# A head step, a kept-weights step, the mixer's bank pairs and the first tiles put in another order in a one-core decoder layer

## The chip, the cores and the metric

The kernel runs on one core of one Trainium2 chip. The metric is the device time of one execution in microseconds (us). The core's engines are named as in its profile: PE (matrix products), PEld (its weight loads), DVE (vector), ACT (scalar, pointwise functions), POOL (general purpose) and SP, which issues most DMAs. Each engine takes its instructions strictly in order.

## The reference

One layer of a decoder on 1040 rows (16 learned rows ahead of 1024 tokens) of 1024 columns, in float32:

```python
u = rmsnorm(h, mix_norm_pre[l])
proj = u @ w_in[l]
q, f_logit, i_in, g_out, v_pool, gate_a, gate_b = jnp.split(proj, cuts, axis=-1)
a = hgrn2(q, f_logit, i_in, g_out, lbs[l], hgrn_out_norm[l])
p = multiscale_pool(v_pool, pool_proj[l], pool_scale[l])
z = (sigmoid(gate_a) * (a @ w_branch_hgrn[l])
     + sigmoid(gate_b) * (p @ w_branch_pool[l]))
h = h + rmsnorm(z @ w_out[l], mix_norm_post[l])
u = rmsnorm(h, ffn_norm_pre[l])
gt = causal_dwconv(u @ ffn_w_gate[l], ffn_conv_w[l], ffn_conv_b[l])
y = (gelu(gt) * (u @ ffn_w_up[l])) @ ffn_w_down[l]
h = h + rmsnorm(y, ffn_norm_post[l])
```

`hgrn2` is a gated linear recurrence over four heads of 128 columns, `multiscale_pool` subtracts each value from trailing means over 2, 4, 8 and 16 rows and multiplies each of four groups by a 128x128 matrix.

## The kernel before

**Products.** Every float32 operand is split into two parts that PE takes at its faster float32 rate: a rounded high part (a cast, on ACT, names ending in `hi` or `h`) and the rest (a subtraction, on DVE, names ending in `lo` or `l`). A product is then three matmuls, high by high, high by low and low by high (`mm3`, lines 221 to 223; in `proj_parts`, lines 241, 242 and 245). So each weight goes DRAM, `wraw`, ACT, DVE, PE, and an operand is ready only when its low part is.

**Stages.** The first tiles (lines 1060 to 1170, to about 60 us): rows of the input are loaded, squared and summed on ACT (`sq`), scaled on DVE (`scaled`, into `un`), transposed on PE (`turn`, line 1097, into a bank `pt`, four 128x128 pieces each), split (`hi_` on ACT, `lo_` on DVE) and multiplied with the columns of `w_in` for the value projection (`mm_`, into the two banks `pv`). The 1024 inner columns are taken as eight groups of 128 (0 to 7, the last arguments of `hi_`, `lo_` and `mm_`); a `turn` makes four groups of one row tile, and the weights come as four blocks of two groups each (`wi_hi`, `wi_lo`; `ha` and `hb` are the two halves of a block). Ahead of it `warm(n)` issues n products of constants (`pj`, line 534) into a bank that nobody reads, and a small transpose (`pp`, line 1070) makes the gains `gcol`. This part is ordered by hand for ACT, DVE and PE: what stands in the code stands so on each engine. After row tiles 0 and 1 the next rows are transposed at line 455.

Then the gates (to about 325 us), the heads and the branch products (325 to 554), the mixer `z @ w_out` (554 to about 655) and the feed-forward part (to the end).

**Heads and branches.** For PE this stage is ordered by hand, by the string `ORDER` (line 56); DVE, ACT and POOL are placed by a scheduler that follows what PE needs. A name in `ORDER` is one item: `h0` to `h3` are the next step of that head's generator `head_steps` (line 690); `PV`, `G` and `PP` are projections (`PP` the pooled ones, product bank `ppp`, evacuated by DVE into `uhi`); `BB` and `BA` are the products of the pooled and of the recurrent branch, 8 column groups each (banks `pbb` and `pba`, evacuated into `sa`), where `a` and `b` are the halves of a product whose inner columns are cut in two; `sa0` to `sa3` split a head's output into `ah` and `al`, the operands of `BA`; `w0` to `w5` each run a step of `keep_first` or `keep_unit`.

A head step begins with a multiply on DVE of every second row of `q` by `f` (line 753), then 32 small products `kb` by `q` into a bank `sb` (line 758), then levels: 32 small products into `sl` (line 735), the last ones `sm` (line 774) and `ms` (lines 837, 838, sums for a normalization).

**Kept weights.** `keep_unit` (line 986) loads two blocks of a feed-forward weight ahead of its stage, forms the sums that a seven-product (Strassen) scheme needs on DVE, splits them (ACT `whi`, DVE `wlo`) and writes the result to DRAM as `kept...`, from where the feed-forward stage loads it. The step numbers: the first makes P1 and P2, the next P6 and P5, the third P3 and P7, the fourth P4.

**Banks.** PSUM has eight banks here. `bank()` takes the next free one of the pool, so where a product lies depends on which tiles were taken ahead of it, and its first matmul waits until the tile that had the bank is evacuated. The mixer stage takes the banks in pairs (`pair`): `R[i]` is a row tile's pair, `m` that of the two learned rows that are needed. At the last BA product a `spare` bank is taken and written once by DVE.

The few lines that the prediction's steps need:

```python
    def warm(n):
        for _ in range(n):
            pe.matmul(junk_bank[:, :P], onesm, ident, start=True, stop=True)
...
        q2, f2 = (t[:, M0:].rearrange("p (b two) -> p b two", two=2) for t in (q, f))
        dve.tensor_tensor(q2[:, :, 1], q2[:, :, 1], f2[:, :, 1], ALU.mult)
        ps = bank("sb")
...
            if (kind, i) == ("BA", KD - 1):
                dve.memset(bank("spare")[:, :1], 0.0)
                z0 = [split_z(0, k) for k in range(ZA)]
...
        for i in (1, "m", 0):
            R[i] = Row(0 if i == "m" else HALO + i * P, HALO if i == "m" else P, pair("pm"))
```

## Time and profile before

| what | us |
|---|---|
| median of 3 runs (1304.87 to 1306.25) | 1305.03 |
| the profiled execution | 1304.06 |
| its span, first to last instruction | 1302.4 |
| PE busy | 1287.9 |
| DVE busy | 963.0 |
| ACT busy | 526.8 |
| POOL busy | 354.1 |

A row of the timeline reads: start and duration in us, engine, line of the code, operation, output <- inputs, shapes, and how many instructions stand together; in brackets how long the engine was idle ahead of it and what ended that. Line 81 is a helper through which all DVE and ACT operations go, so there the names tell the place. Starts of PE's matmuls overlap the end of the one ahead, so that the time of a product is the distance of starts, not its duration. The profiled execution's time is 1.66 us longer than its span; the span is what the rows add up to.

### The profile page before, as it was taken

Reading aid. Unit: us, or ns where it says so; the run is one execution under the profiler, and the core shown is the slowest. Engines: PE = TensorE matmul, PEld = TensorE weight load, DVE = VectorE, ACT = ScalarE, POOL = GpSimd, SP = SyncE. Lnnn points to the kernel's source line nnn. Section 1 sums busy time; section 2 is a strip of 40 time slices with the busy share of each in tenths; the row PEclk is TensorE's granted clock in tenths of the full one; section 3 lists DMA queues with packets and bytes.
Section 4 is the critical chain, followed back from the end, with each engine's and each line's share of the span. In section 5 each row is a group of like instructions: output and inputs, shape, how many; then the busy total and the mean of one; then the engine's idle time right before and its main releaser. Section 6 shows DMA issues by size and latency. Waiting matters only on the chain.

```text
span 1302.4 us, 21989 instructions
## 1 busy us (share of the span) xinstructions
PE 1287.9 (99%) x8651; PEld 1136.6 (87%) x8651; DVE 963.0 (74%) x1312; ACT 526.8 (40%) x918; POOL 354.1 (27%) x308
## 2 busy tenths in 40 slices
PE   8999999999999999999999999999999999999998
PEld 7799899999999898968898888888888888888887
DVE  6768965554776878766688999888898885455758
ACT  7554533332244646235563222222232232444443
POOL 3015333130000000150145555454665552000000
PEclk9999999999999999999999999999999999999999
DMA  7145542325614767866777776667777699666644
GB/s 279 42 107 170 196 158 97 122 90 157 175 61 145 228 227 259 308 194 243 275 251 250 206 212 173 160 184 199 179 177 171 146 262 287 208 226 222 231 170 162
DMA packets 143817, 247.62 MB, mean 190 GB/s; under 512 B 11008, under 2 KB 75180, under 8 KB 143714
## 3 DMA queue, kind: packets, MB, share of 16 engines
q1 hardware_dynamic: 127026, 213.42, 49.1%
q0 software_dynamic: 12064, 24.38, 11.3%
q10 hardware_dynamic: 4624, 8.41, 1.7%
q8 instruction: 68, 1.11, 0.4%
q14 instruction: 35, 0.29, 0.1%
HBM read 174.12 MB, written 95.09 MB: 207 GB/s over the span
## 4 chain that ended last, share of the span: by engine, by line
PE 93%; DVE 2%; ACT 2%; DMA 1%; issue 0%; SPq 0%; POOL 0%; DVEq 0%; ACTq 0%; POOLq 0%
PE P L341 17%; PE P L342 17%; PE P L344 17%; PE pd L221 5%; PE pd L223 5%; PE pd L222 5%; PE pm L221 2%; PE pm L223 2%; PE pm L222 2%; PE ppv L241 1%; PE ppv L245 1%; PE ppv L242 1%; PE pg L241 1%; PE pv L223 1%; PE pg L242 1%; PE pv L221 1%
## 5 line engine op out<-in xcount | busy, mean ns | idle before, releaser
L81 ACT CAST whi<-wraw 128x512 fp32r<-128x512 f32 (+2 forms) x140 | 97.0, 714 | 163.6 <-PE P L342 87.7
L342 PE MATMUL P<-v,whi 128*128 128x512 f32 (+2 forms) x408 | 140.7, 353 | 0.0
L341 PE MATMUL P<-v,whi 128*128 128x512 f32 (+2 forms) x408 | 140.7, 352 | 0.0
L344 PE MATMUL P<-v,wlo 128*128 128x512 f32 (+2 forms) x424 | 135.1, 349 | 0.0
L81 DVE TENSOR_TENSOR p<-p,P 128x512 f32<-128x512 f32 (+2 forms) x122 | 83.3, 683 | 44.1 <-PE P L344 43.2
L81 DVE TENSOR_TENSOR wlo<-wraw,whi 128x512 fp32r<-128x512 f32 (+2 forms) x110 | 95.9, 891 | 11.3 <-ACT whi L81 7.0
L312 POOL TENSOR_TENSOR swa<-wraw,wraw 128x512 f32<-128x512 f32 x32 | 49.3, 1540 | 188.6 <-DMA wraw<-in_w_in_dram 77.1
L81 DVE TENSOR_TENSOR rot<-wraw,rot 128x1024 fp32r<-128x1024 f32 x31 | 37.9, 1224 | 72.3 <-ACT rot L81 72.2
L341 PEld LDWEIGHTS P<-v,whi 128*128 128x128 f32 x408 | 76.7, 188 | 10.5
L342 PEld LDWEIGHTS P<-v,whi 128*128 128x128 f32 x408 | 76.6, 188 | 10.2
L344 PEld LDWEIGHTS P<-v,wlo 128*128 128x128 f32 x424 | 74.0, 188 | 10.8
L223 PE MATMUL pd<-rot 128*128 128x512 f32 x274 | 82.5, 388 | 0.0
L222 PE MATMUL pd<-rot 128*128 128x512 f32 x274 | 82.5, 388 | 0.0
L221 PE MATMUL pd<-rot 128*128 128x512 f32 x274 | 81.9, 388 | 0.1
L81 ACT CAST whi<-swa 128x512 fp32r<-128x512 f32 x64 | 38.1, 619 | 92.3 <-PE P L342 81.8
L81 DVE TENSOR_TENSOR wlo<-swb,whi 128x512 fp32r<-128x512 f32 x64 | 65.9, 1037 | 9.5 <-ACT whi L81 9.5
L81 ACT CAST rot<-wraw 128x1024 fp32r<-128x1024 f32 x31 | 32.7, 1054 | 90.8 <-PE pd L223 89.4
L341 PE MATMUL P<-uhi,whi 128*128 128x258 f32 (+2 forms) x240 | 68.5, 303 | 0.0
L342 PE MATMUL P<-ulo,whi 128*128 128x258 f32 (+2 forms) x240 | 68.4, 303 | 0.0
L81 ACT CAST whi<-swb 128x512 fp32r<-128x512 f32 x64 | 38.1, 618 | 69.3 <-PE P L342 63.3
L341 PE MATMUL P<-t4h,whi 128*128 128x258 f32 (+2 forms) x228 | 65.5, 304 | 0.0
L341 PE MATMUL P<-t2h,whi 128*128 128x258 f32 (+2 forms) x228 | 65.3, 304 | 0.2 <-DVE sg L81 0.2
(354 smaller groups left out, 3751.3 us busy)
## 6 DMA issues: line engine op xcount, KB each, us to landing
wraw<-in_w_in_dram SPq DMA_DIRECT2D x36, 512.0 KB, 5.6
yt<-ysum SPq DMA_DIRECT2D x33, 512.0 KB, 5.2
wraw<-in_ffn_w_gate_dram SPq DMA_DIRECT2D x26, 512.0 KB, 6.5
wraw<-in_ffn_w_up_dram SPq DMA_DIRECT2D x22, 512.0 KB, 6.9
wsum<-in_ffn_w_down_dram SPq DMA_DIRECT2D x22, 512.0 KB, 8.2
wraw<-in_w_out_dram SPq DMA_DIRECT2D x18, 512.0 KB, 6.1
ysum<-ys SPq DMA_DIRECT2D x11, 768.0 KB, 5.8
sa<-sscr SPq DMA_DIRECT2D x16, 513.0 KB, 7.5
```

Of the source, the lines that this page charges most:

```text
L81: self.last = method(*a, **k)
L221: pe.matmul(ps, ahi, bhi, start=first, stop=False)
L222: pe.matmul(ps, ahi, blo, start=False, stop=False)
L223: pe.matmul(ps, alo, bhi, start=False, stop=last)
L241: pe.matmul(ps[:, :n], whi[:, k, :], xhi, start=(k == 0), stop=False)
L242: pe.matmul(ps[:, :n], whi[:, k, :], xlo, start=False, stop=False)
L245: pe.matmul(ps[:, :n], wlo[:, k, :], xhi, start=False, stop=(k == n_k - 1))
L312: pool_e.tensor_tensor(s1, a21, a22, ALU.add)
L341: pe.matmul(d, whi[:, k, :], xh[:, c : c + w], start=(k == 0 and onto is None), stop=False, **go)
L342: pe.matmul(d, whi[:, k, :], xl[:, c : c + w], start=False, stop=False, **go)
L344: pe.matmul(x[:, o : o + w], wlo[:, k, :], xh[:, c : c + w], start=False, stop=(k == 3), **go)
```

## The change

Five edits, none of which changes what is computed:

1. *First tiles*: eleven junk products ahead of the small transpose and two behind it (eight and six before), the copy of `gcol` behind the scaling of row 0, and another order of casts, subtractions, transposes and products.
2. *Head steps*: for heads 0 and 1 the first multiply is issued ahead of the generator's first yield, that is one item earlier in `ORDER`.
3. `ORDER`: head 3's item between `PP3` and `BBa0` moves behind `BBa0`.
4. `ORDER`: a kept-weights step `w5` moves from ahead of `BBb6` to behind `BAa1` (it is the one with P3 and P7).
5. The `spare` bank at the last BA product is gone, and the mixer's pairs are taken in the order m, 0, 1.

```diff
-         "Gr3 h2 PP1 h0 Gs3 h3 PP2 h2 PP3 h3 BBa0 h1 h2 BBb0 h1 h3 w0 BBa1 h2 BBb1 h3 w1 BBa2 h2 BBb2 h3 w2 BBa3 h2 "
+         "Gr3 h2 PP1 h0 Gs3 h3 PP2 h2 PP3 BBa0 h3 h1 h2 BBb0 h1 h3 w0 BBa1 h2 BBb1 h3 w1 BBa2 h2 BBb2 h3 w2 BBa3 h2 "
...
+        q2, f2 = (t[:, M0:].rearrange("p (b two) -> p b two", two=2) for t in (q, f))
+        if h < 2:
+            dve.tensor_tensor(q2[:, :, 1], q2[:, :, 1], f2[:, :, 1], ALU.mult)
         yield
...
-        q2, f2 = (t[:, M0:].rearrange("p (b two) -> p b two", two=2) for t in (q, f))
-        dve.tensor_tensor(q2[:, :, 1], q2[:, :, 1], f2[:, :, 1], ALU.mult)
+        if h >= 2:
+            dve.tensor_tensor(q2[:, :, 1], q2[:, :, 1], f2[:, :, 1], ALU.mult)
...
-        warm(8)
+        warm(11)
         gp = bank("pp")
...
-        dve.tensor_copy(gcol, gp[:, :KD])
-        warm(6)
+        warm(2)
...
         sq(0)
         scaled(0, 0)
+        dve.tensor_copy(gcol, gp[:, :KD])
+        turn(0, 0)
         wi_hi(0, ha)
+        wi_hi(0, hb)
         wi_lo(0, ha)
-        turn(0, 0)
-        hi_(0, 0)
-        lo_(0, 0)
-        wi_hi(0, hb)
         wi_lo(0, hb)
-        hi_(0, 1)
-        lo_(0, 1)
+        hi_(0, 0, 1)
+        lo_(0, 0, 1)
         mm_(0, 0, 1)
...
-                dve.memset(bank("spare")[:, :1], 0.0)
...
-        for i in (1, "m", 0):
+        for i in ("m", 0, 1):
```

What the edits do to the order of instructions, at three places.

ACT in the first tiles, before (`un_228` is row 0's square, `whi_219` and `whi_221` are the first two weight blocks, `pt_237` and `pt_271` the first transposes of rows 0 and 1, `un_261` row 1's square):

```order
L81 CAST whi_219<-wiraw_94 128x512
L81 ACTIVATE uhi_90<-pt_237,gcol_211 128x128
L81 CAST whi_219<-wiraw_94 128x512
L81 ACTIVATE uhi_90<-pt_237,gcol_211 128x128
L81 ACTIVATE un_261,ssq_260<-row_96 128x1024
L81 ACTIVATE std_263<-ssq_260,eps_t 128x1
L81 ACTIVATE uhi_90<-pt_237,gcol_211 128x128 x2
L81 CAST whi_221<-wiraw_98 128x1024
L81 ACTIVATE uhi_90<-pt_271,gcol_211 128x128 x2
```

The same place after (`whi_217` and `whi_219` are now the first two blocks, `pt_234` and `pt_267` the transposes, `un_260` row 1's square):

```order
L81 CAST whi_217<-wiraw_94 128x512 x2
L81 ACTIVATE uhi_90<-pt_234,gcol_214 128x128 x2
L81 ACTIVATE un_260,ssq_259<-row_96 128x1024
L81 ACTIVATE std_262<-ssq_259,eps_t 128x1
L81 ACTIVATE uhi_90<-pt_234,gcol_214 128x128
L81 CAST whi_219<-wiraw_98 128x512
L81 ACTIVATE uhi_90<-pt_234,gcol_214 128x128
L81 CAST whi_219<-wiraw_98 128x512
L81 ACTIVATE uhi_90<-pt_267,gcol_214 128x128 x4
```

Both halves of the first block are cast ahead of row 0's groups 0 and 1, and the second block is cast half by half between its groups 2 and 3. On PE row 1's second transposes move behind two more groups of three products, and `mm_(0, 2)` and `mm_(0, 3)` now stand together ahead of `mm_(1, 0, 1)`.

DVE behind PP3, before (`ppp` are PP3's three banks, `sl_4980` head 3's moved products, `k_4552` and `q_4554` head 3's operands, `f_4375` head 2's):

```order
L81 SCALAR_TENSOR_TENSOR uhi_90<-ppp_4956,par,uhi_90 128x342
L81 TENSOR_TENSOR f_4375<-f_4375 128x66
L81 TENSOR_TENSOR k_4552<-k_4552,f_4551 128x132x4
L81 TENSOR_TENSOR q_4554<-q_4554,f_4551 128x128x4
L81 SCALAR_TENSOR_TENSOR uhi_90<-ppp_4957,par,uhi_90 128x342
L81 COPY_PREDICATED near_4701<-mask_155,sl_4980 128x32x4
```

And after (`sl_5005` is the same head step):

```order
L81 SCALAR_TENSOR_TENSOR uhi_90<-ppp_4956,par,uhi_90 128x342
L81 TENSOR_TENSOR f_4375<-f_4375 128x66
L81 SCALAR_TENSOR_TENSOR uhi_90<-ppp_4957,par,uhi_90 128x342
L81 TENSOR_TENSOR k_4552<-k_4552,f_4551 128x132x4
L81 TENSOR_TENSOR q_4554<-q_4554,f_4551 128x128x4
L81 COPY_PREDICATED near_4701<-mask_155,sl_5005 128x32x4
```

PP3's third evacuation moves ahead of two multiplies of head 3. On PE the 32 products of head 3 move from directly behind PP3 to behind the 18 products of BBa0. In the built program BBa0's banks are 6, 7 and 1 (before 7, 1 and 4); 6 is that of an earlier `sl` of head 3, 7 and 1 are PP2's first two, and 4 is PP2's third, which now goes to the moved `sl`. `sm` has bank 0, PP3's third.

DVE between the two splits of the last heads' outputs, before (`al_5840` and `al_5909` are the low parts of heads 2 and 3, `wlo_5755` and `wlo_5800` are kept weights, the latter P3 and P7, `wlo_5899` are the weights of BA2 and BA3, `pba_5914` is BA0's first bank):

```order
L81 TENSOR_TENSOR al_5840<-o_5593,ah_5839 128x1026
L81 TENSOR_TENSOR wlo_5755<-wlo_5755,whi_5754 128x512
L81 TENSOR_TENSOR wlo_5800<-wraw_5675,wraw_5677 128x512
L81 TENSOR_TENSOR wlo_5800<-wraw_5675 128x512
L81 TENSOR_TENSOR wlo_5755<-wlo_5755,whi_5754 128x512
L81 TENSOR_TENSOR al_5909<-o_5719,ah_5908 128x1026
L81 TENSOR_TENSOR wlo_5800<-wlo_5800,wraw_5675 128x512
L81 TENSOR_TENSOR wlo_5800<-wlo_5800,whi_5799 128x512
L81 TENSOR_TENSOR wlo_5800<-wraw_5677,wlo_5800 128x512
L81 TENSOR_TENSOR sa_5843<-sa_5843,pba_5914 128x342
```

And after (`al_5826`, `al_5895`, `wlo_5945` for P3 and P7, `wlo_5885` for BA2 and BA3, `pba_5900`):

```order
L81 TENSOR_TENSOR al_5826<-o_5593,ah_5825 128x1026
L81 TENSOR_TENSOR wlo_5755<-wlo_5755,whi_5754 128x512 x2
L81 TENSOR_TENSOR wlo_5885<-wraw_5883,whi_5884 128x1024
L81 TENSOR_TENSOR al_5895<-o_5719,ah_5894 128x1026
L81 TENSOR_TENSOR sa_5829<-sa_5829,pba_5900 128x342
L81 TENSOR_TENSOR sa_5829<-sa_5829,pba_5901 128x342
L81 TENSOR_TENSOR sa_5829<-sa_5829,pba_5902 128x342
L81 TENSOR_TENSOR wlo_5945<-wraw_5675,wraw_5677 128x512
```

The low part of BA2's and BA3's weights moves between the two `al`, and all of P3 and P7 moves behind BA0's evacuation. The six operations of P3 and P7 then stand among the evacuations of BA0 to BA2, and the low part of BA4's and BA5's weights, before ahead of BA2's evacuations, stands behind them.

At the seam to the mixer BA7's banks are 2, 6 and 7 (before 7, 5 and 1), and the pairs of the mixer's first rows are (0, 1) for row 0, (6, 7) for row 1 and (4, 5) for m; before, row 0 had (0, 1) too, with bank 1 still BA7's. For head 1's multiply of edit 2 the place on DVE is the same before and after, behind head 0's `f`; head 1's `k` moves behind the next multiply of `q` and the copy from `sb`.

28 lines of the change are left out of this document (15 added, 13 removed), and 4 rows, old and new, of the table ORDER.

## The prediction

> **What bounds the kernel now.** I read the page first, then the list of PE's waits, then the timelines of PE, DVE and ACT at each wait that the change can reach. The page (span; busy time of each engine):
>
> ```profile
> span 1302.4 us, 21989 instructions
> ...
> PE 1287.9 (99%) x8651; PEld 1136.6 (87%) x8651; DVE 963.0 (74%) x1312; ACT 526.8 (40%) x918; POOL 354.1 (27%) x308
> ```
>
> PE is busy in all but 14.5 us. The change takes no product away; it only reorders, so nothing but PE's waits can be won, and a reordering can lose by making new ones. What there is to win stands in the list of PE's waits (line waited for, us in total, times, longest):
>
> ```profile
> PE pba L242 <- DVE al L81: 1.1, 1, 1.1
> PE pbb L241 <- DVE uhi L81: 0.8, 1, 0.8
> PE pm L221 <- DVE sa L81: 0.7, 1, 0.7
> PE pba L245 <- DVE wlo L81: 0.6, 1, 0.6
> PE po L828 <- DVE st L81: 0.5, 2, 0.3
> PE sb L758 <- issue: 0.5, 1, 0.5
> PE pv L221 <- ACT uhi L81: 0.5, 1, 0.5
> PE pt L1097 <- DVE un L81: 0.4, 1, 0.4
> PE pv L223 <- DVE ulo L81: 0.3, 1, 0.3
> PE pv L222 <- DVE wlo L81: 0.2, 1, 0.2
> PE P L341 <- DVE sg L81: 0.2, 1, 0.2
> ```
>
> Each of these is one event of under 1.2 us (the `po` wait two), and together they are 5.8 us. The four `pv`/`pt` waits are the first tiles, `sb` is head 1's first step, `pbb` the first half of BBa0, the two `pba` the BA products, `pm` the mixer's first product; `po` and `P` (in the gates) are not touched. So the question is which of these go, and whether PE, coming earlier, waits for the same engine further on.
>
> **The change part by part.** *A, the first tiles.* PE's rows, and the ACT row from which the longest wait comes:
>
> ```profile
> 5.51 1.60 PE L534 MATMUL pj<-ident,onesm 128*128 128x128 f32 x12
> 8.01 0.50 PE L221 MATMUL pv<-whi,uhi 128*128 128x512 f32 x1 [0.46 <-ACT uhi L81]
> 10.97 0.63 PE L1097 MATMUL pt<-ident,un 128*128 128x128 f32 x4 [0.42 <-DVE un L81]
> 14.89 0.60 PE L1097 MATMUL pt<-ident,un 128*128 128x128 f32 x4
> 15.24 0.48 PE L221 MATMUL pv<-whi,uhi 128*128 128x512 f32 x1
> 22.16 0.39 PE L221 MATMUL pv<-wihi,uhi 128*128 128x512 f32 x1
> 22.84 0.60 PE L455 MATMUL pt<-ident,un 128*128 128x128 f32 x4
> 8.64 1.05 ACT L81 ACTIVATE un<-row 128x1024 f32<-128x1024 f32 x1
> ```
>
> From 22.16 to the transposes of line 455 stand three products, 22.84 - 22.16 = 0.68 us, so one takes 0.227. From 8.01 to 22.84, 14.83 us, stand 48 products (10.9 us) and three groups of four transposes (15.24 - 14.89 = 0.35 us each, 1.05): 12.0 us of work and 2.9 us of waits. In the new order the first product moves little, since the scaled half of row 0 and its transposes stay where they are: 7.9 rather than 8.01, as one small DVE copy now comes behind the scaling. Its six products and row 0's second transposes then run to about 9.6 with nothing between them, because both halves of the first weight block and both groups are split by then. The transposes of row 1 wait for the chain from ACT's square (8.64) over DVE's `un` to PE (10.97); ACT is free for it at 8.1 rather than 8.64, but when row 1's data land, no row shows, so I let it come only 0.1 us sooner: 10.87, a wait of 1.27. Of the next six products (groups 2 and 3) I charge waits of 0.55 us, since their two weight halves follow on ACT and DVE one by one. From there on (about 13.1) 36 products and the last transposes are back to back: row 1's groups 0 and 1 are split ahead, and each later split is put one group of products ahead of its use. The end: 7.9 + 12.0 + 1.27 + 0.55 = 21.7 rather than 22.84, a gain of **1.15 us**. The bounds: if the data of row 1 do not limit, the chain goes with ACT, 0.5 us more (1.65); if each of the three later splits comes a fifth of a microsecond late, 0.6 less (0.55). Nothing behind 22.84 is late next as far as PE's list shows: between here and the heads it has only the 0.2 us of `P`.
>
> The junk products `pj` ahead of it go from 14 to 13, two rather than six of them behind the small transpose. The later `pj` row takes 1.60 us for 12 records, 0.13 each, so the array is at speed before the first tile and products at 8 to 23 us take 0.227 like those at 22. [...]
>
> *B, head 0's and 1's first multiply issued ahead of the yield.*
>
> ```profile
> 334.10 0.75 PE L758 MATMUL sb<-q,kb 128*32 128x32 f32 x64 [0.49 <-issue]
> 333.31 0.69 DVE L81 TENSOR_TENSOR q<-q,f 128x512 f32<-128x512 f32 x1
> ```
>
> PE's `sb` of head 1 waits for DVE's `q<-q,f`, which ends at 334.0. In the order of DVE this multiply stands in the same place as before, directly behind head 0's `f<-f`; what moved is only head 1's `k<-k,f`, behind two of its neighbours. So the wait stays: **0**. The edit does not do there what its words say; the bounds are -0.2 (the `k` is needed by the next step) and the whole 0.5.
>
> *C, head 3's step behind BBa0.*
>
> ```profile
> 434.72 0.42 PE L241 MATMUL pbb<-uhi,whi 128*128 128x342 f32 x1 [0.78 <-DVE uhi L81]
> 438.24 0.24 PE L774 MATMUL sm<-q,k 128*16 128x1 f32 x4
> 439.24 0.42 PE L241 MATMUL pbb<-uhi,whi 128*128 128x342 f32 x1
> 432.39 0.57 DVE L81 SCALAR_TENSOR_TENSOR uhi<-ppp,par,uhi 128x342 fp32r<-128x342 f32 x1
> 438.27 0.57 DVE L81 SCALAR_TENSOR_TENSOR uhi<-ppp,par,uhi 128x342 fp32r<-128x342 f32 x1
> ```
>
> BBa0's third bank is the one that PP2's third evacuation (`uhi<-ppp`) frees, and PE stands 0.78 us for it. With head 3's 32 small products moved behind, `sl` takes that bank and BBa0 gets the one that head 3's earlier step left and PP2's first two. The last of these is free at 432.39 + 0.57 = 432.96, and PE asks for it about then. So that wait goes. What is late next is `sm`, 438.24 in before: its bank is now PP3's third, evacuated in before at 438.27. Two operations of head steps (a multiply of `k` and one of `q`, 0.6 us each as 512 columns take on DVE) come behind that evacuation instead of ahead of it, so it starts at 437.05 and ends at 437.6. `sm` then starts at about 437.6, and BBb0 as far behind it as before (439.24 - 438.24 = 1.0), at 438.6 rather than 439.24: **0.6 us** (0.2 if two thirds of one such operation still stand ahead; 0.95 if `sm` waits no more).
>
> *D, the kept-weights step moved from ahead of BBb6 to behind BAa1.*
>
> ```profile
> 509.72 1.22 DVE L81 TENSOR_TENSOR al<-o,ah 128x1026 fp32r<-128x1026 f32 x1
> 513.27 1.22 DVE L81 TENSOR_TENSOR al<-o,ah 128x1026 fp32r<-128x1026 f32 x1
> 514.54 0.42 PE L242 MATMUL pba<-al,whi 128*128 128x342 f32 x1 [1.13 <-DVE al L81]
> 519.22 1.21 DVE L81 TENSOR_TENSOR wlo<-wraw,whi 128x1024 fp32r<-128x1024 f32 x1
> 520.35 1.34 DVE L81 TENSOR_TENSOR sa<-sa,pba 128x342 f32<-128x342 f32 x3
> 520.49 0.76 PE L245 MATMUL pba<-ah,wlo 128*128 128x342 f32 x3 [0.60 <-DVE wlo L81]
> 524.91 0.63 PE L245 MATMUL pba<-ah,wlo 128*128 128x342 f32 x3
> 532.08 0.63 PE L245 MATMUL pba<-ah,wlo 128*128 128x342 f32 x3
> ```
>
> Between the two `al` DVE has four kept-weights operations (513.27 - 509.72 - 1.14 = 2.4 us). Afterwards two of these stand there (1.2) and the `wlo` of BA2 and BA3 (1.2): the same 2.4 us. So the second `al` ends as late as before and the 1.13 us stay; I take 0.07 for them. But `wlo`, which ended at 520.43 and held BA2 for 0.60 (0.77 against the usual interval of two products), is done at about 513.2: that wait goes. Price of the moved step: the `wlo` of BA4 and BA5 now stands behind BA2's evacuations on DVE. By the rows of before BA2's last products end at 524.91 + 0.63, three evacuations take 1.34 and the `wlo` 1.2, so it is done at 528.1, against its first use at 532.08: 4 us of cover. **0.84 us** (0.3 to 2.0, the upper end if the `al` too comes sooner).
>
> *E, the spare bank gone and the mixer's pairs taken as m, 0, 1.*
>
> ```profile
> 554.20 0.51 DVE L81 TENSOR_TENSOR sa<-sa,pba 128x342 f32<-128x342 f32 x1 [0.45 <-PE pba L223]
> 554.86 0.47 PE L221 MATMUL pm<-whi,zc 128*128 128x512 f32 x1 [0.70 <-DVE sa L81]
> ```
>
> The mixer's first pair lay on a bank of BA7's, and its first product waited 0.70 us for BA7's last evacuation. In the new order BA7 ends on banks 2, 6 and 7 and the first pair is (0, 1), long free; the pair with bank 7 comes six products later (1.36 us), when that evacuation is done. The operands of these products are split well ahead. **0.70 us** (0.5 to 0.75).
>
> The sum: 1.15 + 0 + 0.6 + 0.84 + 0.70 = 3.3 us. The profiled execution took 1304.06 us (span 1302.4 and 1.66 around it), so it becomes 1300.8. The median of the runs, 1305.03, lies 0.97 above it, and the forecast for the median is 1301.7. A difference of 0.2%, 2.6 us, is about what a measurement of this kernel can tell from no change.
>
> **The rivals.** *Given back at the heads.* Kept weights come by DMA and go back by DMA, and DVE, in order, waits for them with the heads' work behind:
>
> ```profile
> 476.50 1.29 DVE L81 TENSOR_TENSOR wlo<-wraw,wraw 128x512 f32<-128x512 f32 x2 [3.90 <-DMA wraw<-in_ffn_w_gate_dram]
> ```
>
> If these trips set the pace, PE's earlier arrival from A and C becomes a longer `po` wait behind them, and D and E alone remain: 1.54 us, 1303.5. For it speaks the 3.9 us of idle time; against it, that each trip starts from a buffer that the earlier work frees, so it starts earlier too. *The second `al` and head 1's `sb` go too* (DVE comes to them with less behind it): 1.13 + 0.49 more, up to 4.9 us; I take 4.4, 1300.6. Against it: the same sum of operations between the two `al`. *Slower: BA4's weights come late.* The moved step holds its two buffers longer, and the loads behind it on SP's queue (BA6's and `w_out`) and on DVE start later. A load takes 6 to 7 us by the page's list of DMA issues; were the `wlo` of BA4 behind one whole trip (8 us with its split), 4 of them would show, and 0.7 us be lost in all: 1305.8. It decides from 4 + 3.3 = 7.3 us of lateness. Against it: the raw weights of BA4 are loaded ahead of the moved step. [...]
>
> **How the numbers follow.** Forecast 0.50, given back 0.29, both more go 0.11, late weights 0.06, clock 0.04. The likeliest is 1301.7. Its own bounds, with one or two terms at their ends, are about 1300.6 to 1302.9. The range goes to 1300.0 below (the case of 4.4 with A at its end) and 1304.1 above (the given-back case with C's lower end); the late weights and the tails are left out, 2 in 10. Faster by over 2.6 us, below 1302.4: four fifths of the forecast and all of the third, 0.51. Slower by over 2.6 us needs 10 us of lateness: 0.04, with what I do not see. The rest, 0.45, is within.
>
> **What would show it.** In the profile after: PE's first transposes of line 455 at 21.7 (A); `sb` still waiting about 0.5 (B); no `pbb` wait for `uhi`, and BBb0 some 1.8 us earlier than 439.24 (A and C); the `al` wait still 1.1 and no `pba` wait for `wlo` (D); no `pm` wait for `sa`, the mixer at about 551.6 (A to E). Wrong it would be if `po` waits for `st` by over 1 us, if a `pba` product of BA4 to BA7 waits for `wlo`, or if the end of the first tiles stays at 22.8.

## The result, and the profile after

The changed kernel takes **1303.73 us** (median of 19 runs, 1301.81 to 1305.96); the kernel before, beside it on the same chips, 1305.88 (19 runs, 1303.55 to 1306.87). The ratio is 0.9985, 95% interval 0.9978 to 0.9992: 2.0 us won, and between 1.0 and 2.9. The forecast was 1301.7 and a gain of 3.3 us. The range held the time and the direction was right; some 0.4 of the forecast gain is missing, and the rest of this text is about where it went.

The page of the profiled execution (1302.24 us, span 1300.5; before 1304.06 and 1302.4), span and busy time:

```profile
span 1300.5 us, 21985 instructions
...
PE 1287.5 (99%) x8649; PEld 1136.7 (87%) x8649; DVE 965.3 (74%) x1311; ACT 527.0 (41%) x919; POOL 355.6 (27%) x308
```

PE is as busy as before; its idle time went from 14.5 to 13.0 us. The list of PE's waits after, without its wait at the very start (line waited for, us in total, times, longest):

```profile
PE pba L242 <- DVE al L81: 1.1, 1, 1.1
PE po L831 <- DVE st L81: 0.9, 2, 0.7
PE sl L738 <- issue: 0.6, 1, 0.6
PE sb L761 <- issue: 0.5, 1, 0.5
PE pv L221 <- ACT uhi L81: 0.5, 1, 0.5
PE P L341 <- DVE sg L81: 0.4, 1, 0.4
PE sm L777 <- DVE uhi L81: 0.2, 1, 0.2
PE pt L1099 <- ACT whi L81: 0.2, 1, 0.2
```

All the waits that the sum counted on are gone (`pbb`, `pm`, `pba` for `wlo`, and `pt` and the later `pv` of the first tiles), those that it left are there (`al`, `sb`), and three are new: `sl` stands 0.6 us for "issue", that is, for nothing that the profile shows, and `sm` and another `pt` stand 0.2 us each. `po` and `P` have grown. Such a list says what went, not how much reached the end. For that I follow the places on PE's timeline whose rows of before the prediction shows, or whose starts of before are given below:

```profile
21.89 1.80 PE L455 MATMUL pt<-ident,un 128*128 128x128 f32 x15
...
138.74 0.36 PE L341 MATMUL P<-t2h,whi 128*128 128x272 f32 x1 [0.37 <-DVE sg L81]
...
435.59 0.42 PE L840 MATMUL ms<-rh,onesr 128*128 128x342 f32 x1
...
438.47 0.44 PE L738 MATMUL sl<-q,k 128*32 128x16 f32 x30 [0.63 <-issue]
438.84 0.42 PE L241 MATMUL pbb<-uhi,whi 128*128 128x342 f32 x1
...
489.62 0.49 PE L831 MATMUL po<-q,st 128*128 128x128 f32 x2 [0.74 <-DVE st L81]
...
514.50 0.42 PE L242 MATMUL pba<-al,whi 128*128 128x342 f32 x1 [1.08 <-DVE al L81]
...
553.07 0.39 PE L221 MATMUL pm<-whi,zc 128*128 128x512 f32 x1
```

| place on PE | before | after | ahead by | ahead by the forecast |
|---|---|---|---|---|
| end of the first tiles (L455) | 22.84 | 21.89 | 0.95 | 1.15 |
| gates, `P` of L341 | 139.26 | 138.74 | 0.52 | 1.15 |
| behind BBa0, first `ms` | 437.02 | 435.59 | 1.43 | no row forecast |
| first product of BBb0 | 439.24 | 438.84 | 0.40 | 1.75 |
| head 2's `po` | 489.59 | 489.62 | none | 1.75 |
| BA0's first `al` product | 514.54 | 514.50 | 0.04 | 1.8 |
| mixer's first product | 554.86 | 553.07 | 1.79 | 3.3 |
| span | 1302.4 | 1300.5 | 1.9 | 3.3 |

So edits 1 and 3 did win time where they stand, and by 489 us all of it was lost again: 0.43 by 139, 1.03 between 435.6 and 438.8, 0.4 at `po`. Edit 4 and the seam to the mixer then won theirs. Each of these losses has its own row. But first the gain at 22.84 itself, for the profile of before was a lucky one there.

*The first tiles: a stretch that is shorter, behind a start that varies.* Of the kernels run below two have the first tiles of before. One of them, `de_only`, in the same places:

```profile
5.95 2.35 PE L534 MATMUL pj<-ident,onesm 128*128 128x128 f32 x12
...
9.19 0.50 PE L221 MATMUL pv<-whi,uhi 128*128 128x512 f32 x1 [0.46 <-ACT uhi L81]
...
24.03 1.14 PE L455 MATMUL pt<-ident,un 128*128 128x128 f32 x9
```

The twelve records of junk products (two for each product) that took 1.60 us in before took 2.35 here, and everything behind them is 1.2 us later. PE begins at 2.03 us (2.04 in `de_only`), the records of its junk products start 0.21 us apart, and from some moment on 0.11, which is called "at speed" below: at 4.93 us in before, 7.58 in `de_only`, 6.22 in after. Over 14 profiles:

| | array at speed from | first product | end (L455) | first product to end |
|---|---|---|---|---|
| order of before (3 kernels) | 4.93, 7.58, 7.97 | 8.01, 9.19, 9.36 | 22.84, 24.03, 24.20 | 14.84 in all |
| order of edit 1 (11 kernels) | 5.54 to 8.19 | 8.07 to 9.25 | 21.54 to 22.75 | 13.47 to 13.53 |

What sets this moment no row shows. It lies 2.9 to 6.2 us behind PE's first junk product, and kernels with the same first tiles differ in it: by 3.0 us with the order of before, by 2.65 with that of edit 1. The profile's windows print a granted clock of 1.00 here too, but only because they take 1.00 where nothing is recorded: the trace's own list of the granted clock begins at this moment, with 1.00 from 4.88 us on in before and 6.18 in after, 0.05 and 0.04 us ahead of the first short distance. So what edit 1 wins is steady, 1.34 us from the first product to the end, while the start moves with this moment, by 1.35 us between the earliest and the latest of the 14 profiles (8.01 and 9.36). Before's profile had the earliest of all.

*Lost by 139 us: one DVE operation that met one of POOL's.* DVE, then POOL, before:

```profile
110.65 0.55 DVE L81 TENSOR_SCALAR fk<-fk,oml,lb 128x528 f32<-128x528 f32 x1 [0.71 <-ACT fk L81]
111.24 1.42 DVE L81 TENSOR_SCALAR fk<-fk 128x528 f32<-128x528 f32 x1
...
110.85 1.52 POOL L312 TENSOR_TENSOR swa<-wraw,wraw 128x512 f32<-128x512 f32 x1 [3.56 <-DMA wraw<-in_w_in_dram]
```

and after:

```profile
109.61 1.62 DVE L81 TENSOR_SCALAR fk<-fk,oml,lb 128x528 f32<-128x528 f32 x1 [0.71 <-ACT fk L81]
111.26 1.42 DVE L81 TENSOR_SCALAR fk<-fk 128x528 f32<-128x528 f32 x1
...
109.64 1.29 POOL L312 TENSOR_TENSOR swa<-wraw,wraw 128x512 f32<-128x512 f32 x1 [3.40 <-DMA wraw<-in_w_in_dram]
```

The same operation takes 0.55 us where POOL starts 0.2 us behind it and 1.62 where POOL starts with it; the one behind it runs beside POOL in both kernels and takes 1.42 in both. DVE, 1.04 us ahead at 109.6, is level at 111.25. Some of that comes back, and PE waits 0.37 us for `sg` at 138.74, where it waited 0.16:

```profile
139.26 0.36 PE L341 MATMUL P<-t2h,whi 128*128 128x272 f32 x1 [0.16 <-DVE sg L81]
```

Over the 14 profiles the split is clean: in the five where POOL started 0.20 to 0.34 us behind the operation it took 0.55 to 0.56, and in the nine where POOL was at work or started within 0.07 us of it, 1.44 to 1.66. What is more, in all nine the operation ends 0.29 to 0.30 us behind the end of POOL's (111.23 against 110.93 in after), whenever it began; and in all five POOL's ends 1.71 to 1.72 us behind the start of DVE's. So the rows read as if the one that comes second waited until the first is done, rather than both running slower. POOL starts there when a load lands ("<-DMA wraw"), so it is a race, and before's profile is one of the five that won it. What the two engines share no row shows; the price of one such meeting is 1.1 us (1.62 against 0.55).

*Lost at 438 us: PE's own instructions.* The 64 products of `sl` break behind the 34th, and no operand or bank is missing. The DMA table of the trace has a queue of instructions (q8: 68 transfers, 1.11 MB, so 16 KB each; for PE's 17298 products and weight loads that is one for each 254). Two stretches of after, from the start of PE's block of instructions to 0.1 us ahead of the transfer, and with it (transfers, MB, share of 16 engines):

```profile
q1 hardware_dynamic: 1277, 1.38, 103.0%
...
q1 hardware_dynamic: 602, 0.42, 101.2%
q8 instruction: 1, 0.02, 5.2%
```

Between 431.7 and 435.7 us the 16 DMA engines are full of loads and no instructions come; the 16 KB come at 435.81 to 436.89, and PE goes on at 438.47. In PE's records (products, weight loads and its 233 semaphore records, counted in order) the breaks of this stretch stand at numbers 7617, 7873 and 8129, 256 apart, in every kernel that has them, whatever the order of the work in between: at the edges of blocks of instructions. That is a reading, and experiments below test it. Not all of the 1.03 us is the break. From the first `ms` to the first `sm` PE takes 1.22 us in before and 1.68 in after, where its starts (436.04, 436.52 and 437.27) follow the ends of DVE's evacuations of PP3's banks (435.98, 436.46 and 437.12): 0.46 us, in pieces of which the list has only the 0.2 of `sm`. The other 0.57 is the break.

*Lost at 489 us: a kept-weights step.* DVE before, then after:

```profile
483.85 0.34 DVE L81 SCALAR_TENSOR_TENSOR st<-st,f,ds 128x128 f32<-128x128 f32 x1
484.12 0.69 DVE L81 TENSOR_TENSOR wlo<-wraw,wraw 128x512 f32<-128x512 f32 x1
...
483.23 0.34 DVE L81 SCALAR_TENSOR_TENSOR st<-st,f,ds 128x128 f32<-128x128 f32 x1
484.15 0.69 DVE L81 TENSOR_TENSOR wlo<-wraw,wraw 128x512 f32<-128x512 f32 x1 [0.58 <-DMA kept5l<-wlo]
```

DVE is 0.6 us ahead of before here (483.23 against 483.85), waits 0.58 us until a store of kept weights has freed its buffer, and is then 0.03 behind (484.15 against 484.12); `st`, for which `po` waits, stands behind it. This is the mechanism of the rival "given back at the heads", with a price of 0.4 us.

### The profile page after: what moved, and what is told of

It is laid out like the page before. It is cut to its first block, busy times and chain, and to the rows that moved or that the text cites. A ratio compares the mean times of both kernels' runs of the same rounds, so it can differ in the third digit from the quotient of the medians.

```text
span 1300.5 us, 21985 instructions
## 1 busy us (share of the span) xinstructions
PE 1287.5 (99%) x8649; PEld 1136.7 (87%) x8649; DVE 965.3 (74%) x1311; ACT 527.0 (41%) x919; POOL 355.6 (27%) x308
## 3 DMA queue, kind: packets, MB, share of 16 engines
q8 instruction: 68, 1.11, 0.3%
## 4 chain that ended last, share of the span: by engine, by line
PE 94%; DVE 2%; ACT 2%; DMA 1%; issue 1%; POOL 0%; DVEq 0%; POOLq 0%
PE P L341 17%; PE P L342 17%; PE P L344 17%; PE pd L221 5%; PE pd L223 5%; PE pd L222 5%; PE pm L221 2%; PE pm L222 2%; PE pm L223 2%; PE ppv L241 1%; PE ppv L245 1%; PE ppv L242 1%; PE pg L241 1%; PE pv L222 1%; PE pg L242 1%; PE pv L221 1%
## 5 line engine op out<-in xcount | busy, mean ns | idle before, releaser
L341 PE MATMUL P<-v,whi 128*128 128x512 f32 (+2 forms) x408 | 140.7, 352 | 0.0
L341 PEld LDWEIGHTS P<-v,whi 128*128 128x128 f32 x408 | 76.7, 188 | 10.5
L341 PE MATMUL P<-uhi,whi 128*128 128x258 f32 (+2 forms) x240 | 68.6, 303 | 0.1
L341 PE MATMUL P<-t2h,whi 128*128 128x258 f32 (+2 forms) x228 | 65.3, 304 | 0.4 <-DVE sg L81 0.4
L341 PE MATMUL P<-t4h,whi 128*128 128x258 f32 (+2 forms) x228 | 65.5, 304 | 0.0
```

Source lines behind the costliest of these rows:

```text
L341: pe.matmul(d, whi[:, k, :], xh[:, c : c + w], start=(k == 0 and onto is None), stop=False, **go)
```

## The experiments

The theory that these rows suggest: D and E count, A and C are given back at the heads. The rival: A and C count too, and the profile of one execution, with its chance collisions, hides it. "Place" numbers below are PE's starts against the profile of before, "ahead" meaning earlier.

**ac_only and de_only: the change in two halves.** `ac_only` is before with edits 1 and 3, `de_only` before with edits 4 and 5. Edit 2 is in neither. Their lines beside those of edit 1, which `ac_only` has whole:

```diff
 ac_only
-"... h2 PP3 h3 BBa0 h1 h2 BBb0 ..."
+"... h2 PP3 BBa0 h3 h1 h2 BBb0 ..."
 de_only
-"... BBa6 h2 w5 BBb6 ... BAa0 BAa1 BAb0 ..."
+"... BBa6 h2 BBb6 ... BAa0 BAa1 w5 BAb0 ..."
-        for i in (1, "m", 0):
+        for i in ("m", 0, 1):
-                dve.memset(bank("spare")[:, :1], 0.0)
```

> The kernel before with only the new first tiles (A) and head 3's step behind BBa0 (C). Given-back theory: PE is about 1 us early at 24 us and up to 0.8 us early at 434, but stands at the same time as before at 493, so the span is that of before within 0.2 us and the ratio 1.000. Rival (A and C count, D and E only partly): the span 1.2 to 1.7 us shorter, ratio 0.9988.

> The kernel before with only the kept-weights step moved (D) and the spare bank gone with the pairs in the new order (E). Given-back theory: as the changed kernel, 1.8 us shorter in the span (0.9 at 520, 0.9 at 554), ratio 0.9986. Rival: 0.3 to 0.7 us shorter, ratio 0.9996.

Measured: `ac_only` 1303.5 us (11 runs) against 1305.18, ratio 0.9988 (0.9979 to 0.9996); `de_only` 1304.65, ratio 0.9994 (0.9985 to 1.0003). My theory had it the other way round and falls; the rival is nearer. The two gains, 1.6 and 0.8 us, add up to 2.4, which fits the 2.0 of the whole. The traces show why A and C get more and E less than expected. The mixer's first product in `ac_only`, and in `de_only`:

```profile
554.62 0.39 PE L221 MATMUL pm<-whi,zc 128*128 128x512 f32 x1
```

```profile
555.63 0.47 PE L221 MATMUL pm<-whi,zc 128*128 128x512 f32 x1 [0.70 <-DVE sa L81]
```

The wait of 0.70 us is gone in the half that has not got edit 5, and is there in the half that has it. Also, `ac_only` breaks longer in `sl` than after does:

```profile
439.19 0.44 PE L735 MATMUL sl<-q,k 128*32 128x16 f32 x30 [1.30 <-issue]
```

It was 0.84 us ahead at the first `ms` (436.18) and is 0.32 behind at BBb0's first product (439.56). In `de_only` PE, late from its start on, is 1.71 us behind before ahead of the second `al` and 0.77 behind from 521.57 (in before) on: 0.94 won there, 0.05 of it at `al`.

**late_w4 and h2_behind: the two losses of the heads, one each.** Both are the kernel after with one line of `ORDER` changed: kept-weights steps one group later, and head 2's step moved behind BBb0.

```diff
 late_w4
-"... BBa4 w4 BBb4 h2 h3 w4 BBa5 sa0 w5 BBb5 h3 sa1 w5 BBa6 h2 BBb6 ..."
+"... BBa4 BBb4 h2 h3 w4 BBa5 sa0 w4 BBb5 h3 sa1 w5 BBa6 h2 w5 BBb6 ..."
 h2_behind
-"... PP3 BBa0 h3 h1 h2 BBb0 h1 h3 ..."
+"... PP3 BBa0 h3 h1 BBb0 h2 h1 h3 ..."
```

> The changed kernel with the kept-weights steps w4 and w5 each one or two items later, so that no kept-weights operation stands among DVE's st operations before 492. Given-back theory (DVE's st chain behind a kept-weights store sets the po waits at 489): the po waits for st go (0.9 us of idle time, 1.5 us of lost starts) and PE is 0.5 us or more ahead of before at 493; if nothing new waits at the al of head 3, the span is 1.0 to 1.5 us shorter than the changed kernel's. Rival (the po wait is set by the heads' own operations): the po waits stay.

> The changed kernel with head 2's step moved from ahead of BBb0 to behind it, so that the small products do not come at 437. Instruction-fetch theory (PE stood 0.63 us at 438.47 because its next 16 KB of instructions, fetched from 435.8, were not in): no such stall, PE about 0.8 us further at 441 than in the changed kernel, and given back at 489. Rival (the stall is head 2's data): it moves with the products and stays about as long.

Measured: `late_w4` 1301.89 us (1300.73 to 1304.46), ratio to before 0.9979 (0.9970 to 0.9988); `h2_behind` 1302.46 (1301.21 to 1304.11), also 0.9979 (0.9970 to 0.9988). The two longest of PE's waits in `late_w4`:

```profile
PE sl L738 <- issue: 1.3, 1, 1.3
PE pba L242 <- DVE al L81: 0.8, 1, 0.8
...
```

The `po` wait, 0.9 us in after, is not in the list any more, though `sl` still breaks, so the kept-weights step is the cause of that loss: PE, 0.25 us behind before at BBb0, is 1.20 ahead at 492.5, where after went from 0.40 ahead to level. In `h2_behind` the break moves:

```profile
PE pm L221 <- DVE sa L81: 0.7, 1, 0.7
...
PE pbb L245 <- issue: 0.4, 1, 0.4
```

`sl` no longer breaks, and PE is 1.80 us ahead at 442.27; but at the next edge of 256 records, in the middle of a BB product, it stands for "issue" and is 1.25 ahead behind it. Its `po` wait is 0.5 us as in before, and PE is 1.13 us ahead there, so the gain was not given back at 489 as expected. The wait of the mixer for `sa` is back: the moved step turns the banks once more. Both kernels' ratios lie below after's 0.9985, but their intervals overlap with its.

**c_only, a_only, no_c: whose is the bank at the mixer, and whose the break.** `c_only` is before with edit 3 alone (one word of `ORDER`), `a_only` with edit 1 alone, `no_c` is after without edit 3.

```diff
 c_only, against before
-"... PP3 h3 BBa0 h1 h2 BBb0 ..."
+"... PP3 BBa0 h3 h1 h2 BBb0 ..."
 no_c, against after
-"... PP3 BBa0 h3 h1 h2 BBb0 ..."
+"... PP3 h3 BBa0 h1 h2 BBb0 ..."
```

> The kernel before with only head 3's step behind BBa0 (C). Bank theory: one bank taken later turns the order of the banks, so the last BA product ends on bank 7 and the mixer's first product does not wait (0.9 us won at 554), though the spare bank and the pairs are as before. Fetch theory: the small products of heads 3 and 2 come within 3 us and PE stands 0.6 to 1.5 us at one of its 256-instruction block starts at 437 to 439, which takes all that the bank wait at 434 gave. Together 0 to 1 us faster. Rival for the bank: the pm wait of 0.7 us stays.

> The kernel before with only the new first tiles (A). PE 1.0 to 1.2 us ahead at 24 us. Given-back theory: of this 0 to 0.5 us is left at 493, where DVE's st operations stand behind a kept-weights store, and the median is 0 to 0.5 us lower. Rival (A counts whole): 1.0 us lower, ratio 0.9992.

> The changed kernel with head 3's step back ahead of BBa0 (A, B, D and E, no C). Bank theory: the pm wait of 0.7 us for sa is back, though the spare bank is gone and the pairs are in the new order. Fetch theory: no wait of PE for issue at 437 to 439, the pbb wait for uhi of 0.8 to 1.1 us is back. Span 0.5 to 1.0 us longer than the changed kernel's, between 1301.0 and 1301.5. Rival (C only cost at 437): shorter than the changed kernel's.

Measured, against 1305.47 (27 runs): `c_only` 1304.34, 0.9995 (0.9986 to 1.0004); `a_only` 1304.17, 0.9992 (0.9983 to 1.0001); `no_c` 1304.39, 0.9993 (0.9984 to 1.0001). No one of them can be told from before, and what they tell is in the traces. (The first tiles of `a_only` end only 0.40 us ahead of before's, at 22.44, as its array is at speed from 7.55 on.) The mixer's first product in `c_only`:

```profile
554.93 0.39 PE L221 MATMUL pm<-whi,zc 128*128 128x512 f32 x1
```

and in `no_c`:

```profile
555.85 0.47 PE L221 MATMUL pm<-whi,zc 128*128 128x512 f32 x1 [0.70 <-DVE sa L81]
```

With edit 3 and without 5 no wait, with 5 and without 3 the full 0.70 us. In the built programs BA7's last bank is 1, one of row 0's pair, in before, `de_only` and `no_c`, and 7 in after, `ac_only` and `c_only`: the moved head step turns the rotation of the banks, and by chance BA7 ends on another. And in `a_only`, which has the order of before in the heads:

```profile
PE sl L735 <- DVE uhi L81: 0.9, 1, 0.9
PE sl L735 <- issue: 0.8, 1, 0.8
```

PE comes there 0.27 us behind before, stands at records 7617 and 7873, 1.14 and 0.97 us between two starts, and is 1.27 behind at BBb0. `no_c` does the same:

```profile
PE sl L738 <- issue: 0.8, 1, 0.8
```

So both expectations from the instructions missed: `c_only`, which was to stand 0.6 to 1.5 us at an edge at 437 to 439, stands 0.15 there, and `no_c`, which was to run through, stands 0.97, with a span of 1303.3 us for 1301.0 to 1301.5. These stands are no matter of edit 3; they come with edit 1. The name "DVE uhi" on the first of `a_only`'s is the profile's guess: it is on the same record as the others.

**no_e: after without edit 5.**

```diff
+                dve.memset(bank("spare")[:, :1], 0.0)
...
-        for i in ("m", 0, 1):
+        for i in (1, "m", 0):
```

> The kernel after without edit 5: the spare bank's memset is back and the mixer's pairs are taken as 1, m, 0. As on record, the spare bank was what put a bank of BA7's into the mixer's first pair: then pm waits 0.7 us for sa again and the ratio to before is 0.9990 (1.3 us less won of 1302). Theory now (edit 3 turns the rotation of the banks by one tile and frees the pair, edit 5 does nothing): no pm wait for sa, the mixer as far ahead of before as in the kernel after (1.6 to 2.0 us), ratio 0.9985 as after.

Measured: 1302.79 us (10 runs, 1300.98 to 1304.07) against 1305.38, ratio 0.9978 (0.9968 to 0.9987).

```profile
553.01 0.39 PE L221 MATMUL pm<-whi,zc 128*128 128x512 f32 x1
```

No wait, and the mixer within 0.06 us of after's 553.07. Edit 5 does nothing here.

**gate_less and gates_out: the loads in front of the instructions.** Both are the kernel after without loads of BB gates, two of them and five (there `m in (0, 1, 2, 3, 4)`):

```diff
     def load_gate(d, b, m):
         d[m] = slot(TQ, name="sa")
+        if b and m in (3, 4):
+            return
...
+            if d is sbs and m in (3, 4):
+                dve.tensor_copy(d[m][:, lo : lo + n], ps[:, :n])
+                continue
```

> The kernel after, but the gates of BB3 and BB4 are not loaded (two transfers of 513 KB out of the crowd of 425 to 436 us) and their evacuations copy the banks instead of multiplying by the gate; PE's instructions and their order are the same. It is a look, not a version. Theory (PE stands in mid-sl at 438.47 because its next block of instructions is fetched late behind the loads): the 16 KB instruction transfer that ran at 435.81 to 436.89 comes at least 0.7 us sooner after PE's stop at 432, and the 0.63 us of idle time on sl (issue) falls under 0.3. Rival (sl waits for an operand or a bank after all): the transfers of instructions may move, but sl stands 0.5 to 0.8 us as before, since none of its operands comes sooner.

> The kernel after, but the gates of BB0 to BB4 are not loaded (five transfers of 513 KB, about 7 us of all 16 engines) and their evacuations copy the banks instead of multiplying; a look, not a version. Taking out the last two of them alone thinned the DMA engines only behind 439 us, so the place at stake stayed full. Now 432 to 437 us should be thin (a share under 0.6 in its middle). Theory (the block of instructions comes late because the loads are ahead of it): the 16 KB transfer that started 4.1 us behind the stop at 432 starts at most 2.5 us behind it, and the idle time on sl (issue), 0.6 us after and 1.2 with two gates out, goes under 0.3. Rival (the delay of that transfer does not hang on the loads): it starts 3.5 us or more behind the stop again, and sl stands 0.5 to 1.3 us.

`gate_less` missed: the transfer came 4.05 us behind the block's start as before, and `sl` stood longer.

```profile
440.20 0.44 PE L738 MATMUL sl<-q,k 128*32 128x16 f32 x30 [1.22 <-issue]
```

But the loads left out were the last in the queue, and the place at stake stayed full. Its window from the block's start to the transfer (the last column but one is the DMA share, 1.06):

```profile
433.50:437.50 4.00, 3.90 (x83) 3.69 (x84) 4.00 (x9) 2.57 (x4) 0.00 (x0) 1.00 1.06 348
```

So it took nothing away there and decided nothing. `gates_out` did: its windows from the block's start on,

```profile
431.90:433.30 1.40, 1.31 (x8) 1.34 (x9) 1.40 (x3) 1.40 (x4) 0.00 (x0) 1.00 0.04 10
433.30:434.30 1.00, 1.00 (x9) 1.00 (x8) 1.00 (x3) 0.98 (x2) 0.00 (x0) 1.00 0.06 16
```

the DMA queue in 433.2 to 434.4, and PE at `sl`:

```profile
q8 instruction: 1, 0.02, 5.0%
```

```profile
436.89 0.74 PE L738 MATMUL sl<-q,k 128*32 128x16 f32 x62
```

(The two kernels took 1306.48 and 1302.27 us in one run each, with part of the work left out.) With the engines empty the transfer starts 1.4 us behind the block's start, and `sl` runs through. The theory holds, on one profile of a kernel that leaves these loads out. In numbers, for the block from record 7617 to 7873:

| kernel | block starts | 16 KB of instructions | next block starts | block took | stand at its end |
|---|---|---|---|---|---|
| before | 431.81 | 435.72 to 436.82 | 438.84 | 7.03 | 0.01 |
| after | 431.74 | 435.81 to 436.89 | 438.47 | 6.73 | 0.81 |
| ac_only | 432.41 | 436.57 to 437.64 | 439.19 | 6.78 | 1.49 |
| c_only | 433.10 | 437.18 to 438.29 | 439.59 | 6.49 | 0.15 |
| a_only | 433.48 | 437.59 to 438.79 | 440.14 | 6.66 | 0.97 |
| no_e | 432.19 | 436.44 to 437.65 | 438.94 | 6.75 | 1.40 |
| gate_less | 433.49 | 437.54 to 438.76 | 440.20 | 6.71 | 1.40 |
| gates_out | 431.88 | 433.30 to 434.26 | 437.18 | 5.30 | 0.01 |

(The stand is the distance between the starts of two records, of which the profile counts some 0.2 us as work.) Under these loads the block takes 6.5 to 7.0 us. In before, BBa0's wait for its bank, 0.78 us, fell in the same block, the transfer ended 2.02 us ahead of the next one, and PE did not stand. The cost, where PE stood in `sl`, was 0.6 to 1.3 us.

The other edges of the 14 profiles add two things. A full share of the DMA engines does not by itself delay the transfer so much: in the two blocks ahead of this one, with shares as high, it started 0.5 to 2.8 us behind the block's start (in after 0.75 us at a share of 1.07 and 1.85 at 1.09), so the share alone does not tell the delay, and what else does, no row here takes apart. And PE's going on follows the end of the transfer closely: of the edges between 425 and 446 us PE stood 0.3 us or more at 21, in 12 of the 14 profiles, and at each went on 1.28 to 1.62 us behind the transfer's end.

**late_h2p: the three repairs together.** After with the lines of `late_w4` and `h2_behind`, and one pair of banks skipped ahead of the mixer, so that the pairs do not meet BA7's last bank:

```diff
+        dve.memset(pair("spare")[:, :1], 0.0)
         for i in ("m", 0, 1):
```

> The changed kernel with the kept-weights steps later (as late_w4), head 2's step behind BBb0 (as h2_behind), and one pair of banks taken and written ahead of the mixer's, so that its first pair is not on the bank that the last BA product leaves. No po wait for st, no pm wait for sa, at 437 to 445 at most 0.5 us for issue: span about 1298.5, 1.0 us shorter than late_w4's 1299.6, median about 3.5 us below the kernel before. Rival (what one place gives the al of heads 2 and 3 take back): the span not below 1299.6.

Measured: **1300.31 us** (5 runs, 1299.4 to 1301.38) against 1305.47, ratio 0.9961 (0.9949 to 0.9974), the fastest here; the interval lies below after's. Its longest waits:

```profile
PE pba L242 <- DVE al L81: 0.8, 1, 0.8
PE pbb L241 <- DVE uhi L81: 0.7, 1, 0.7
PE pba L241 <- ACT ah L81: 0.5, 1, 0.5
...
```

No `po`, no `pm`, no break in `sl`. What is left at 432.31 ("DVE uhi") stands on record 7617, the edge ahead.

**h2p_junk: the edges moved back.** That edge takes 0.8 to 1.3 us in nine of the ten kernels so far with edit 1 and up to 0.24 in the three without. Edit 1 issues one junk product less, four records and a semaphore's. Here it is put back:

```diff
-        warm(11)
+        warm(12)
```

> late_h2p with one junk product more ahead of the small transpose (twelve instead of eleven), so that the edges of PE's instruction blocks fall at the same places of the work as in the kernel before. In nine of ten kernels with edit 1 PE stands 0.8 to 1.3 us between the records 7616 and 7617 (0.9 in late_h2p, at 432.2 us), in the three with the first tiles of before 0.0 to 0.24. Theory: edit 1 issues two products and two weight loads fewer, the edge falls behind PP3's last products instead of between them, and that makes the stand; with the junk product back it is under 0.3 us, the wait of pbb at 432 goes, and the time is 0.2 to 0.7 us below late_h2p's ratio of 0.9961 (0.9957), less 0.1 to 0.2 us for the junk product if the array is late at speed. Rival: the edge's place does not matter, the 16 KB come 2.4 to 2.8 us behind the block's start because the loads are ahead of them; the stand stays 0.7 to 1.3 us and the ratio is 0.9961 to 0.9963.

Measured: 1300.16 us (5 runs, 1299.6 to 1300.93) against 1305.44, ratio 0.9964 (0.9951 to 0.9978): no change to `late_h2p`. The trace says why. Its longest waits:

```profile
PE pba L242 <- DVE al L81: 0.8, 1, 0.8
PE pbb L242 <- issue: 0.8, 1, 0.8
...
```

At record 7617 the distance of two starts falls from 0.89 to 0.36 us, and the `pbb` wait at 432 is gone, nearly as the theory has it; PE is 0.64 us ahead of `late_h2p`, of which 0.1 it was before. But at record 8129 the distance grows from 0.41 to 1.08, and by 444.5 it is 0.2 behind. So the place of the edges in the work matters, and what is won at one is asked back two edges on, where the transfer is late as well.

## Why the prediction was right or wrong

**A, first tiles: right, and mis-sized on the low side; wrong in what follows.** The end came at 21.89 for 21.7, 0.95 us for 1.15. But the working took the start of before's profile, 8.01, as given: "In the new order the first product moves little" holds if PE is at speed from the same moment on, and that moment lay anywhere from 5.54 to 8.19 us in kernels with the new first tiles. From the first product on edit 1 wins 1.34 us where the sum had 1.0 (14.83 us made into 13.8). The next step failed: "Nothing behind 22.84 is late next as far as PE's list shows". The list shows who waits, not who would wait, and 0.43 us was gone by 139 us, in a stretch where one DVE operation lost 1.07 us to POOL. More went to PE's instructions: with one junk product less their edges fall elsewhere, and `a_only` stands 1.1 us at one where the kernels with the old first tiles stand at most 0.24; the table under C has the price. In the medians edit 1 alone is 0.9992 (0.9983 to 1.0001), between nothing and 2.2 us.

**B: right.** `sb` waits 0.5 us as before; the edit does not do there what its words say.

**C: right for the edit alone, wrong in the whole change.** The wait of `pbb` for its bank went, and `ms` and `sm` were late next, for PP3's evacuations, much as forecast. But I looked for the next lateness among banks and DVE operations only, and it was PE's instruction block, behind loads that the page counts in one line of 68 transfers. What that takes depends on where edit 1 puts the edges. PE's time from PP3's last product of line 242 (431.58 in before) to BBb0's first (439.24), for the kernels with all loads and head 2's step in place:

| | without edit 3 | with edit 3 |
|---|---|---|
| first tiles of before | 7.66 (before), 7.69 (`de_only`) | 7.05 (`c_only`) |
| edit 1 | 8.66 (`a_only`), 8.65 (`no_c`) | 7.77 (after), 8.36 (`no_e`), 8.42 (`late_w4`), 8.95 (`ac_only`) |

Alone, edit 3 wins the 0.6 us that the sum had; alone, edit 1 loses 1.0 here; together they lose 0.1 to 1.3, and the profile of after, with the least, is the luckiest of four with this order. In return edit 3 won 0.9 us at the mixer, by the rotation of the banks, which I had put down to edit 5.

**D: right.** 0.84 us forecast; PE is 0.04 us ahead at the second `al` and 0.93 ahead behind BA2's `wlo`; 0.94 won in `de_only`. The `al` wait stayed at 1.08 for 1.13. The cover was smaller than worked out: the `wlo` of BA4 and BA5 was done at 529.0 instead of 528.1, against a first use that came 0.9 earlier, so some 2 us instead of 4. It held.

**E: the place and the size right (0.70 forecast, 0.9 won between 551 and 555), the cause wrong.** The step that failed is "In the new order BA7 ends on banks 2, 6 and 7", which I gave to edit 5. It is true of the changed program, but three kernels show that edit 3 does it and edit 5 nothing: `c_only`, `no_e` and `no_c`. That the term came out is luck: the sum of the whole change did not suffer, and a forecast for its parts would have.

**The rivals.** "Given back at the heads" named 1303.5 and the median is 1303.73, but that is luck, for it was the wrong account of it: its own mechanism took 0.4 us of the 1.75, and A and C do reach the medians (`ac_only` 0.9988). "The second `al` and head 1's `sb` go too" and "BA4's weights late" did not come. The term "clock 0.04" among the chances no run shows: in after the record of the granted clock stands at 1.00 from 6.18 us on, so also in the window of the first products (granted clock in the last column but two):

```profile
7.50:10.00 2.50, 2.04 (x11) 1.32 (x9) 1.82 (x5) 1.98 (x6) 0.28 (x1) 1.00 1.05 393
```

**The step from span to median.** The sum was made against one profile: before's lay 1.8 us below the median that 19 runs gave (1304.06 and 1305.88), after's 1.5 below (1302.24 and 1303.73). I had taken 0.97 from three runs, and 0.85 us of the 2.03 us by which the forecast missed the median are that. The rest, some 1.2, is the gain: 2.15 us between the medians for 3.3. That before's profile was so far below has causes in the trace. It had won the race at 110 us, and its array was at speed 2.7 and 3.0 us sooner than in the two other kernels with its order, and its first tiles ended 1.2 and 1.4 us sooner.

**What stays open.** No kernel was made that keeps POOL away from DVE at 110 us, so that collision is read from the order of starts and ends in 14 profiles and not shown by an experiment, and what the rest of the way to 139 us owes to it is not known. Between the end of the first tiles and the place of 139.26 five kernels won it (before, and four that gained 0.15 to 0.36 us on before); of the nine that lost it eight lost 0.12 to 0.55 and one, `c_only`, gained 0.24. What else moves there was not taken apart. That the edges are what edit 1 loses at 432 to 439 us is shown in part: `h2p_junk` puts them back and the stand at 7617 falls from 0.89 us to 0.36, but no kernel moves the edges and nothing else of edit 1 with head 2's step in place.

## What to carry to other kernels

Where PE is busy 99% of the time, a wait that is removed is won only if what comes next is early too, and the list of waits names only the last to come: ask of each stretch what else ends close behind, the engine's own instructions among it, for which PE stood up to 1.3 us here at one edge of a block, between loads that filled the DMA engines (shares of 1.02 to 1.09). A move of one item turns every rotation behind it, of banks as of buffers, so what a seam far down wins or loses belongs to whatever changed the count; the banks of the built program, and a kernel with one edit alone, tell which. And a gain or a loss in one profile can be chance, of the moment from which PE is at speed (4.93 to 8.19 us here) or of a load that lands (0.55 or 1.62 us for one operation): with gains of a thousandth the medians of ten or more runs decide, and profiles of several kernels that share a stretch say what it takes.

## What the runs showed of the hardware

- PE's instructions come in transfers of 16 KB, one for each 254 products and weight loads (256 records between the breaks). In the block from record 7617, with the 16 DMA engines full (shares of 1.02 to 1.09), the transfer started 3.9 to 4.3 us behind the block's start, and with them empty (0.04, one profile) 1.4 us; it took 1.0 to 1.2 us. In the two blocks ahead it started 0.5 to 2.8 us behind, at shares as high. At each of the 21 edges of this stretch at which it stood 0.3 us or more, PE went on 1.28 to 1.62 us behind the transfer's end. The profile calls the break "issue", or names an engine that is no cause.
- The records of junk products at the kernel's start ran 0.21 us apart and then 0.11, from a moment 2.9 to 6.2 us behind the first of them in 14 profiles, and with it PE's first product moved between 8.01 and 9.36 us. The trace's list of the granted clock begins 0.05 (before) and 0.04 us (after) ahead of that moment, with 1.00; a window ahead of it prints 1.00 as well.
- A DVE operation on 128x528 elements took 0.55 us where POOL started 0.2 us or more behind it, and 1.44 to 1.66 where POOL was at work or started with it (14 profiles); there it ended 0.29 to 0.30 us behind POOL's operation in all nine.
